# Queries, keys and latents of two attentions computed with tokens on the partitions, in a two-layer hybrid block

## The chip, the cores and the metric

The kernel runs on one core of a Trainium2 chip. The metric is device microseconds of one execution. A profiled execution gives busy times, waits and the granted TensorE clock. TensorE multiplies matrices; VectorE (DVE), ScalarE (ACT) and GpSimd (POOL) work elementwise; SyncE (SP) starts the weights' transfers and POOL's queue starts the others.

## The reference, cut to what matters

256 tokens, width 2048, float32. A first layer (forgetting attention and an RWKV scan) is followed by a second layer, the block that the change touches:

```python
h = rms_norm(x, norm_g)
proj = h @ w_in                     # split into c_q, c_kv, k_rope_raw, mem_q, conv parts, gates
q = (rms_norm(c_q, q_norm_g) @ w_uq).reshape(b, s, 16, 128 + 64)
q_nope = rms_norm(q[..., :128], qn_nope_g)
q_rope = apply_rope(rms_norm(q[..., 128:], qn_rope_g), cos, sin)
kv = (rms_norm(c_kv, kv_norm_g) @ w_ukv).reshape(b, s, 16, 128 + 128)
k_nope, v = rms_norm(kv[..., :128], kn_nope_g), kv[..., 128:]
k_rope = apply_rope(rms_norm(k_rope_raw, kn_rope_g), cos, sin)
p = softmax(where(allowed, (q_nope @ k_nope.T + q_rope @ k_rope.T) * scale, -inf))
# memory: 4 heads of 256
mq = rms_norm(mem_q.reshape(b, s, 4, 256), qn_g)
mk, mv = split(rms_norm(mem, mem_norm_g) @ w_mem_kv); mk = rms_norm(mk, kn_g)
x = x + merged @ w_o                # merged: the gated sum of convolution, MLA and memory
```

A norm here is over the 512 channels of a latent, the 128 or 64 of a head's part, or the 256 of a memory head.

## The kernel before

All weights stream from HBM in 658 blocks of 128x1024 in a fixed order (`weight_groups`, L27). For each block `conv_to` makes two copies, `whi` (ScalarE, L278) and `wlo = raw - whi` (VectorE, L241); activations are kept as such pairs too, and a product is three matmuls in fp32r: high by high, high by low, low by high. Four blocks of `whi`/`wlo` exist at a time, and they are made three blocks ahead of TensorE.

`gemm` (L478) runs one group, 512 output columns of a projection, over its k-tiles of 128. It has two forms. With `tm` set (tokens on the partitions) the activations of 128 tokens are the stationary operand and 512 weight columns stream: two accumulators, six matmuls of 128x512 per k-tile. Without it (channels on the partitions) 128 weight columns are stationary and 256 tokens stream: four accumulators, twelve matmuls of 128x256 per k-tile. All matmuls through the helper `mm` carry L286. Five banks of PSUM hold accumulators, three serve everything else (`bank`).

The small work is written as generators (`spawn`): `gemm` calls `pump` between its matmuls, which advances the jobs while a simple clock of the engines says that there is room; the compiler then orders each engine's queue. So norms and attention lie between the weight matmuls.

Before the change the groups `mk`, `cq`, `ckv`, `krope`, `mq`, `qr`, `qn` and `kn` have channels on the partitions. Their norms are then sums over partitions: `head_rs` (L603) splits the squares into a pair, sums with eight `hs` matmuls against selectors, takes the reciprocal root on 128x256 (`rsqrt`, eleven VectorE steps), and brings the factors to all partitions by a round trip through DRAM on POOL's queue (`hd`, then `hr`). `mem_norm` and `nope_norm` (L1563) multiply by it, `q_rope_all` (L1613) and `rope_job` also rotate: `rotate` copies half-rows across partitions by DMA (`rot`) and combines with tables `cos` and `sin`. `latent_job` (L1438) sums with `mm(ps, ones, r)` (`lss`). In the stretch after `mz` the memory attention (`ms`, softmax `mx` and `msm`, transposes `mpt`, `mpo`), the MLA heads (`ls`, `sm`, `lpt`, `lpo`) and the causal convolution (`cg`, its shifted copies `ul` by DMA, its weights `cw`) run as jobs between the groups.

Of the kernel before, what the change touches and what calls it, by code (L numbers as in the profile page):

```python
# [26 lines left out]
def weight_groups():  # L27
# [29 lines left out]
    for j in range(2):  # L57
        add(f"mk{j}", "w_mem_kv_2", 2048, _tiles(512 * j, 4))
# [22 lines left out]
    for b in range(2):  # L81
        add(f"mq{b}", w, 2048, _tiles(7232 + 512 * b, 4))
# [144 lines left out]
def hybrid_kernel(ctx: ExitStack, tc: tile.TileContext, io, out):  # L227
# [301 lines left out]
    def to_pair(x, pair, gain=None):  # L529

        for i in range(2):
# [14 lines left out]
            yield  # L546

# [55 lines left out]
    def head_rs(sq, which, scale, eps, op=ALU.add):  # L603
# [1214 lines left out]
```

## Time and profile before

| | us |
|---|---|
| median of 3 runs (range) | 2023.71 (2021.61 to 2027.49) |
| the profiled execution, its span | 2022.89, 2021.0 |
| the groups `mk` to `mq`, first matmul to last | 838.5 to 1031.5 |
| the heads' groups `qr`, `qn`, `kn` and their attention, first to last | 1077.9 to about 1660 |
| granted TensorE clock | 0.999 |

A page of the profile lists each engine's busy time, the chain of work that ended last, and groups of instructions. A row of a timeline has the start, the length, the engine, the line, the operation, out<-in, the shape and, in brackets, how long the engine had stood idle and for whom. Matmul lengths overlap; the step from start to start is what one costs.

### The profile page before, as it was taken

The page shows a single profiled execution, that of the slowest core. Times are in us where ns is not written, and L with a number is a line of the kernel's source. Part 1 is how long each engine was busy: PE and PEld are TensorE (multiplying, and loading weights), DVE is VectorE, ACT ScalarE, POOL GpSimd, SP SyncE. Part 2 cuts the span into 40 slices and gives each one's busy share as a digit, 9 for nine tenths or more (in the row PEclk, how much of TensorE's full clock was granted, in tenths as well). Part 3 has the DMA queues.
Part 4 walks back from the last instruction along what each step waited for, and adds up shares of the span by engine and source line. Part 5 has one row for each costly group of instructions (what it writes and reads, how often), then busy time and mean ns, then how long its engine had stood idle before and what let it go on. Part 6 is the DMA issues. An engine that isn't in the chain of part 4 may idle for free. (4 is left out here: it accounts for less than half of the span.)

```text
span 2021.0 us, 31907 instructions
## 1 busy us (share of the span) xinstructions
PE 2004.6 (99%) x12702; PEld 1778.0 (88%) x12702; DVE 1305.3 (65%) x2005; ACT 977.3 (48%) x1330; POOL 82.1 (4%) x149
## 2 busy tenths in 40 slices
PE   9999999999999999999999999999999999999999
PEld 9999999898778888899999888888888889988887
DVE  8776847878446568656856675575765755555554
ACT  6734445454444545555445445445545444444432
POOL 0002000020100000000000100100000000000000
PEclk9999999999999999999999999999999999999999
DMA  8454544536546666565555655565665555566564
GB/s 274 162 180 155 196 136 139 179 119 202 174 157 236 229 201 201 191 214 195 182 182 186 189 193 184 181 226 166 198 208 167 188 177 171 193 210 211 192 200 146
DMA packets 106820, 378.52 MB, mean 187 GB/s; under 512 B 13178, under 2 KB 14162, under 8 KB 106672
## 3 DMA queue, kind: packets, MB, share of 16 engines
q1 hardware_dynamic: 97136, 350.11, 52.5%
q0 software_dynamic: 9104, 25.78, 4.4%
q8 instruction: 99, 1.62, 0.3%
q10 hardware_dynamic: 432, 0.61, 0.1%
q14 instruction: 49, 0.40, 0.1%
HBM read 367.32 MB, written 5.86 MB: 185 GB/s over the span
## 5 line engine op out<-in xcount | busy, mean ns | idle before, releaser
L241 DVE TENSOR_TENSOR wlo<-raw,whi 128x1024 fp32r<-128x1024 f32 (+1 forms) x659 | 801.9, 1222 | 559.1 <-ACT whi L278 552.4
L278 ACT ACTIVATE whi<-raw 128x1024 fp32r<-128x1024 f32 (+1 forms) x659 | 695.3, 1058 | 828.7 <-PE acc.lo L286 51.1
L286 PE MATMUL acc.lz<-h2l,whi 128*128 128x256 f32 x256 | 72.5, 284 | 0.0
L286 PE MATMUL acc.lz<-h2h,whi 128*128 128x256 f32 x256 | 72.4, 283 | 0.0
L286 PE MATMUL acc.lz<-h2h,wlo 128*128 128x256 f32 x256 | 72.1, 284 | 0.0
L286 PE MATMUL acc.gm<-wlo,h2h 128*128 128x512 f32 x128 | 50.0, 391 | 1.1 <-DVE wlo L241 1.1
L286 PE MATMUL acc.gb<-wlo,hh 128*128 128x512 f32 x128 | 50.0, 390 | 0.6 <-DVE wlo L241 0.6
L286 PE MATMUL acc.ga<-whi,hl 128*128 128x512 f32 x128 | 50.5, 394 | 0.0
L286 PE MATMUL acc.ga<-wlo,hh 128*128 128x512 f32 x128 | 50.4, 394 | 0.0
L286 PE MATMUL acc.gc<-wlo,h2h 128*128 128x512 f32 x128 | 50.2, 392 | 0.0
L286 PE MATMUL acc.gm<-whi,h2l 128*128 128x512 f32 x128 | 50.2, 392 | 0.0
L286 PE MATMUL acc.gl<-wlo,h2h 128*128 128x512 f32 x128 | 50.1, 392 | 0.0
L286 PE MATMUL acc.gc<-whi,h2l 128*128 128x512 f32 x128 | 50.1, 391 | 0.0
L286 PE MATMUL acc.ga<-whi,hh 128*128 128x512 f32 x128 | 50.0, 392 | 0.0
L286 PE MATMUL acc.gl<-whi,h2h 128*128 128x512 f32 x128 | 50.0, 392 | 0.0
L286 PE MATMUL acc.wo<-wlo,mh 128*128 128x512 f32 x128 | 49.9, 390 | 0.0
L286 PE MATMUL acc.w<-wlo,mgh 128*128 128x512 f32 x128 | 49.9, 390 | 0.0
L286 PE MATMUL acc.w<-whi,mgh 128*128 128x512 f32 x128 | 49.9, 390 | 0.0
L286 PE MATMUL acc.gc<-whi,h2h 128*128 128x512 f32 x128 | 49.9, 390 | 0.0
L286 PE MATMUL acc.wo<-whi,ml 128*128 128x512 f32 x128 | 49.9, 390 | 0.0
L286 PE MATMUL acc.gl<-whi,h2l 128*128 128x512 f32 x128 | 49.8, 389 | 0.0
L286 PE MATMUL acc.w<-whi,mgl 128*128 128x512 f32 x128 | 49.8, 389 | 0.0
(658 smaller groups left out, 5894.5 us busy)
## 6 DMA issues: line engine op xcount, KB each, us to landing
raw<-in_W SPq DMA_DIRECT2D x657, 512.0 KB, 3.5
hr<-hd POOLq DMA_DIRECT2D x10, 512.0 KB, 5.4
hr<-hd POOLq DMA_DIRECT2D x12, 256.0 KB, 4.4
xr<-in_xtm POOLq DMA_DIRECT2D x4, 512.0 KB, 6.3
mt<-in_memT POOLq DMA_DIRECT2D x4, 512.0 KB, 7.0
xbd<-x1g POOLq DMA_DIRECT2D x4, 512.0 KB, 3.9
xo<-xbd POOLq DMA_DIRECT2D x4, 512.0 KB, 4.9
out_tm<-xo SPq DMA_DIRECT2D x8, 256.0 KB, 4.8
```

What stands on the lines that cost most here:

```text
L241: DVE.tensor_tensor(out=o, in0=a, in1=b, op=op)
L278: ACT.activation(out=o, in_=a, func=f, scale=scale, **kw)
L286: TE.matmul(o, lhsT=l, rhs=r, start=start, stop=stop)
```

## The change

The groups named above, but for `krope`, get the `tm` form. Their rows are evacuated by `evac_rows` as two 128x512 copies. A norm is `tm_norm`: squares on ScalarE, a VectorE reduction along the row, `rsqrt` on a few numbers per partition, a broadcast product. The result goes back to channels on the partitions by TensorE transposes (`to_channels`, for the latents the existing `to_pair`), which apply the gain while the bank is read. The rotation `turn` works along the row with tables `rope` that hold gain and scale. `krope` keeps its form, with 64 instead of 128 (doubled) weight columns, and `rope_job` transposes it to tokens and back.

```diff
-        add(f"mk{j}", "w_mem_kv_2", 2048, _tiles(512 * j, 4))
+        add(f"mk{j}", "w_mem_kv_2", 2048, _tiles(512 * j, 4), tm=True)
...
-    add("cq", w, 2048, _tiles(4096, 4))
-    add("ckv", w, 2048, _tiles(4608, 4))
-    add("krope", w, 2048, [[(5120, 64), (5120, 64)]])
+    add("cq", w, 2048, _tiles(4096, 4), tm=True)
+    add("ckv", w, 2048, _tiles(4608, 4), tm=True)
+    add("krope", w, 2048, [[(5120, 64)]])
...
-                [[(192 * (8 * (h // 2) + 2 * i + e) + 128, 64) for e in range(2)] for i in range(4)])
-        add(f"qn{h}", "w_uq_2", 512, [[(192 * (4 * h + i), 128)] for i in range(4)])
-        add(f"kn{h}", "w_ukv_2", 512, [[(256 * (4 * h + i), 128)] for i in range(4)])
+                [[(192 * (8 * (h // 2) + 2 * i + e) + 128, 64) for e in range(2)] for i in range(4)], tm=True)
+        add(f"qn{h}", "w_uq_2", 512, [[(192 * (4 * h + i), 128)] for i in range(4)], tm=True)
+        add(f"kn{h}", "w_ukv_2", 512, [[(256 * (4 * h + i), 128)] for i in range(4)], tm=True)
...
+        width = sum(n for t in e["tiles"] for _, n in t)
...
-                        wh = hi_t[b][:, i * cols:(i + 1) * cols]
-                        wl = lo_t[b][:, i * cols:(i + 1) * cols]
+                        wh = hi_t[b][:, i * cols:i * cols + width]
+                        wl = lo_t[b][:, i * cols:i * cols + width]
                         ah = pairs[k // 4][0][:, k % 4, 128 * t:128 * t + 128]
                         al = pairs[k // 4][1][:, k % 4, 128 * t:128 * t + 128]
-                        mm(acc[t], ah, wh, start=k == 0, stop=False)
-                        mm(acc[t], ah, wl, start=False, stop=False)
-                        mm(acc[t], al, wh, start=False, stop=k == kt - 1)
+                        o = acc[t][:, :width]
+                        mm(o, ah, wh, start=k == 0, stop=False)
+                        mm(o, ah, wl, start=False, stop=False)
+                        mm(o, al, wh, start=False, stop=k == kt - 1)
                         if i == per - 1:
                             pump()
                     if ks[-1][2] == kt - 1:
-                        evac(t, acc[t])
+                        evac(t, acc[t][:, :width])
...
+    def tm_norm(x, d, eps):
+        n = fsz(x) // d
+        v = x if len(x.shape) == 2 else x.rearrange("p t c -> p (t c)")
+        sq = a4("tsq").rearrange("p a b -> p (a b)")[:, :n * d]
+        act(sq, v, AF.Square)
+        r = b1("tn").rearrange("p (k n) -> p k n", k=4)[:, :, :n]
+        ms, y, t, g = (r[:, k, :] for k in range(4))
+        red(ms, sq.rearrange("p (n d) -> p n d", d=d), ALU.add)
+        yield
+        ts(ms, ms, 1.0 / d, ALU.mult, eps, ALU.add)
+        yield from rsqrt(ms, y, t, g)
+        yield SOFT
+        v = v.rearrange("p (n d) -> p n d", d=d)
+        mul(v, v, y.unsqueeze(2).to_broadcast([128, n, d]))
+        yield
+    def to_channels(x, dst, gain):
+        for i in range(2):
+            ps = bank("tc").rearrange("p (c t) -> p c t", c=2)
+            for c in range(2):
+                for t in range(2):
+                    o = 256 * i + 128 * c
+                    TE.transpose(ps[:, c, 128 * t:128 * t + 128], in_=x[:, t, o:o + 128], identity=cc("ident"))
+                    clock["pe"] += 0.11
+            yield
+            for c in range(2):
+                acopy(dst[:, 2 * i + c, :], ps[:, c, :], scale=gain(2 * i + c))
+            yield
+    def evac_rows(d, b, name):
+        t4 = tm4(out4(name))
+        d[b] = t4
+        return lambda t, ps: acopy(t4[:, t, :], ps)
...
-        gemm(f"mk{b}", memn, evac_copy(mk, b, "mk"))
+        gemm(f"mk{b}", memn, evac_rows(mk, b, "mk"))
     def mem_norm(d, gain):
-        sum4 = a4("mks")
         for b in range(2):
-            sq = a4("mksq")
-            act(sq, d[b], AF.Square)
-            yield
-            s4 = sq.rearrange("p (a c) b -> p a c b", c=2)
-            add(sum4[:, 2 * b:2 * b + 2, :], s4[:, :, 0, :], s4[:, :, 1, :])
-        yield from head_rs(sum4, 1, 1.0 / 256.0, 1e-6)
-        y = head_rs.out
-        for b in range(2):
-            t4 = d[b].rearrange("p (a c) b -> p a c b", c=2)
-            for c in range(2):
-                stt(t4[:, :, c, :], t4[:, :, c, :], gain(c), y[:, 2 * b:2 * b + 2, :], ALU.mult, ALU.mult)
-            yield
+            yield from tm_norm(d[b], 256, 1e-6)
+            t = a4("mc")
+            yield from to_channels(d[b], t, lambda c: gain(c % 2))
+            d[b] = t
...
+        gr = b1("gr").rearrange("p (k c) -> p k c", k=4)
         nc.gpsimd.dma_start(out=pos, in_=io["pos"])
-        yield from lag()
-        a, k, r = b1("ang"), b1("ak"), b1("ar")
-        vcopy(a, pos)
-        ts(a, a, cc("invf"), ALU.mult)
+        nc.gpsimd.dma_start(out=gr[:, 0:3, :], in_=io["ropeg"])
+        yield from lag(2 * LAG)
+        w = b1("ang").rearrange("p (k c) -> p k c", k=4)
+        a, k, r, pf = (w[:, i, :] for i in range(4))
...
+        act(r, r, AF.Sin)
+        act(k, k, AF.Sin)
+        ts(gr[:, 0, :], gr[:, 0, :], 192.0 ** -0.5, ALU.mult)
+        for i in range(2):
+            for j, tab in enumerate((k, r)):
+                for e in range(2):
+                    o = slice(32 * e, 32 * e + 32)
+                    mul(rope[:, i, j, :, o], tab.rearrange("p (t f) -> p t f", t=2),
+                        gr[:, i, o].unsqueeze(1).to_broadcast([128, 2, 32]))
+            yield
+    def turn(x, i, n):
+        v = x.rearrange("p t (n c) -> p t n c", c=64)
+        b = a4("turn").rearrange("p a b -> p (a b)")[:, :128 * n].rearrange("p (t n c) -> p t n c", t=2, c=64)
+        tab = lambda j: rope[:, i, j, :, :].unsqueeze(2).to_broadcast([128, 2, n, 64])
+        mul(b, v, tab(1))
+        mul(v, v, tab(0))
+        yield
+        sub(v[:, :, :, 0:32], v[:, :, :, 0:32], b[:, :, :, 32:64])
+        add(v[:, :, :, 32:64], v[:, :, :, 32:64], b[:, :, :, 0:32])
+        yield
...
     def latent_job(d, gain, name):
-        t = d[0]
-        ps = bank("lss")
-        sq = a4("lsq")
-        act(sq, t, AF.Square)
-        r = b1("lr")
-        fold(sq, r, 0)
-        yield
-        mm(ps[:, :256], ones, r)
-        yield
-        ms = b1("lms")
-        ts(ms, ps[:, :256], 1.0 / 512.0, ALU.mult, 1e-6, ALU.add)
-        y, tmp, g = b1("ly"), b1("lt"), b1("lg")
-        yield from rsqrt(ms, y, tmp, g)
-        for c in range(4):
-            stt(t[:, c, :], t[:, c, :], pc(gain, c), y, ALU.mult, ALU.mult)
-        yield
+        x = d[0]
+        yield from tm_norm(x, 512, 1e-6)
         p = new_pair(name)
-        split(t, p[0], p[1])
         lat[name] = [p]
+        yield from to_pair(x, p, lambda c: pc(gain, c))
...
-    def rope_job(x, n, gain, out):
...
+    def rope_job(x):
+        k = b1("kr").rearrange("p (t c) -> p t c", t=2)
+        ps = bank("kr")[:, 0:128]
+        for t in range(2):
+            TE.transpose(ps[:, 64 * t:64 * t + 64], in_=x[:, 128 * t:128 * t + 128], identity=cc("ident", 0, 64, 0, 64))
+            clock["pe"] += 0.11
+        yield
+        x = b1("krn")
+        acopy(x[:, 0:128], ps)
+        yield from tm_norm(x[:, 0:128], 64, 1e-6)
+        yield from turn(x[:, 0:128].rearrange("p (t c) -> p t c", t=2), 1, 1)
+        for e in range(2):
+            vcopy(k[:, :, 64 * e:64 * e + 64], x[:, 0:128].rearrange("p (t c) -> p t c", t=2))
...
-    def rotate(x, n, out):
-        s = a4("rot")[:, 0:n, :]
-        for e in range(4):
-            p = 32 * e
-            q = 32 * (e ^ 1)
-            POOL.dma_start(out=s[p:p + 32, :, :], in_=x[q:q + 32, :, :])
-        yield from lag()
-        cb = lambda a: a.unsqueeze(1).to_broadcast([128, n, 256])
-        mul(s, s, cb(sin))
-        yield
-        mul(x, x, cb(cos))
-        yield
-        add(out, x, s)
...
-    def nope_norm(t, gain):
-        sq = a4("nsq")
-        act(sq, t, AF.Square)
-        yield
-        yield from head_rs(sq, 1, 1.0 / 128.0, 1e-6)
-        stt(t, t, gain, head_rs.out, ALU.mult, ALU.mult)
-        yield
     def mla_job(g):
-        qt, kt_, o = qn[g], kn[g], a4("mo")
+        qt, kt_, o = a4("qc"), a4("kc"), a4("mo")
         lo[g] = o
-        yield from nope_norm(qt, qns[:, 0:1])
-        yield from nope_norm(kt_, pc("kn_g"))
+        for x, t, gain in ((qn[g], qt, qns[:, 0:1]), (kn[g], kt_, pc("kn_g"))):
+            yield from tm_norm(x, 128, 1e-6)
+            yield from to_channels(x, t, lambda c: gain)
...
-        t = qr.pop(g)
-        sq = a4("rsq")
-        act(sq, t, AF.Square)
-        yield
-        yield from head_rs(sq, 0, 1.0 / 64.0, 1e-6)
-        stt(t, t, qns[:, 1:2], head_rs.out, ALU.mult, ALU.mult)
-        yield
-        yield from rotate(t, 4, t)
-        yield
-        qr[g] = []
-        for e in range(2):
-            p, o = slice(64 * e, 64 * e + 64), slice(64 - 64 * e, 128 - 64 * e)
-            x = a4("qro", F32R)
-            acopy(x[p, :, :], t[p, :, :])
-            sub(x[o, :, :], t[p, :, :], x[p, :, :].bitcast(F32))
-            qr[g].append(x)
-            yield
+        x = qr.pop(g)
+        yield from tm_norm(x, 64, 1e-6)
+        yield from turn(x, 0, 8)
+        both = [a4("qro", F32R) for _ in range(2)]
+        for i in range(2):
+            ps = bank("tc").rearrange("p (c t) -> p c t", c=2)
+            for c in range(2):
+                for t in range(2):
+                    o = 256 * i + 128 * c
+                    TE.transpose(ps[:, c, 128 * t:128 * t + 128], in_=x[:, t, o:o + 128], identity=cc("ident"))
+                    clock["pe"] += 0.11
+            yield
+            cs = slice(2 * i, 2 * i + 2)
+            for e in range(2):
+                p, o = slice(64 * e, 64 * e + 64), slice(64 - 64 * e, 128 - 64 * e)
+                acopy(both[e][p, cs, :], ps[p, :, :])
+                sub(both[e][o, cs, :], ps[p, :, :], both[e][p, cs, :].bitcast(F32))
+            yield
+        qr[g] = both
...
-            gemm(f"qr{g // 2}", lat["cq"], evac_copy(qr, g // 2, "qr"))
+            gemm(f"qr{g // 2}", lat["cq"], evac_rows(qr, g // 2, "qr"))
             jq[g // 2] = spawn(q_rope_all(g // 2))
-        gemm(f"qn{g}", lat["cq"], evac_copy(qn, g, "qn"))
-        gemm(f"kn{g}", lat["ckv"], evac_copy(kn, g, "kn"))
+        gemm(f"qn{g}", lat["cq"], evac_rows(qn, g, "qn"))
+        gemm(f"kn{g}", lat["ckv"], evac_rows(kn, g, "kn"))
```

The order of the queues shows the move. On TensorE, at the latents: `lss` of the first latent stood among the 128x256 matmuls of `ckv` (`h2h`, `h2l`: the activations).

```order
L286 MATMUL acc.ckv_9870<-h2l_8847,whi_9863 128x256
L286 MATMUL acc.ckv_9870<-h2h_8846,wlo_9864 128x256
L286 MATMUL lss_9879<-lr_9882,one_84 128x256
L286 MATMUL acc.ckv_9871<-h2h_8846,whi_9863 128x256
L286 MATMUL acc.ckv_9871<-h2l_8847,whi_9863 128x256
```

The same place after the change (`con`: the identity):

```order
L286 MATMUL acc.ckv_9577<-whi_9637,h2l_8880 128x512
L286 MATMUL acc.ckv_9577<-whi_9637,h2h_8879 128x512
L538 MATMUL tr_9706<-con,cq_9351 128x128 x4
L286 MATMUL acc.ckv_9577<-wlo_9638,h2h_8879 128x512
L286 MATMUL acc.ckv_9577<-whi_9637,h2l_8880 128x512
```

The sum over partitions is gone, four transposes of the normed latent stand there, and the streams are twice as wide.

On VectorE, at the first memory head's softmax, before (`qr`: the rotated query part, `hr`: its factors from DRAM):

```order
L1153 TENSOR_REDUCE mx_11709<-ms_11685 128x1 x2
L261 SCALAR_TENSOR_TENSOR qr_11293<-qr_11293,qns,hr_11641 128x1024
L1158 RECIPROCAL mx_11709<-mx_11709 128x2
L255 TENSOR_SCALAR msm_11708<-msm_11708,mx_11709 128x256 x2
L241 TENSOR_TENSOR wlo_11715<-raw_11621,whi_11714 128x1024
```

And after (`tn`: the few numbers of a norm):

```order
L1191 TENSOR_REDUCE mx_11163<-ms_11121 128x1
L241 TENSOR_TENSOR tn_11129<-tn_11129 128x8
L257 TENSOR_SCALAR tn_11129<-tn_11129 128x8
L241 TENSOR_TENSOR tn_11129<-tn_11129 128x8
L241 TENSOR_TENSOR qn_10792<-qn_10792,tn_11129 128x1024
L241 TENSOR_TENSOR wlo_11171<-raw_11041,whi_11170 128x1024
L1196 RECIPROCAL mx_11163<-mx_11163 128x2
L255 TENSOR_SCALAR msm_11162<-msm_11162,mx_11163 128x256 x2
```

The product that needed `hr` no longer stands between `mx` and `msm`; the end of a norm's chain and one weight's `wlo` do.

On POOL's queue, up to the first convolution, before:

```order
L622 DMA hd_11501<-hy_11435 4x256
L623 DMA hr_11502<-hd_11501 128x1024
L625 DMA hd_11640<-hy_11575 8x256
L627 DMA hr_11641<-hd_11640 64x4x256 x2
L1495 DMA rot_11759<-qr_11293 32x1024 x4
L1522 MEMSET ul_12064 1x512
L1522 MEMSET ul_12065 2x512
L1525 DMA cw_12062<-in_cwt 128x1024
L1526 DMA cw_12063<-in_cwt 128x512
L1524 DMA ul_12064<-cg_11615 1x16x32
L1524 DMA ul_12065<-cg_11615 2x512
```

And after:

```order
L1441 DMA pos_9377<-in_pos 128x2
L1442 DMA gr_9378<-in_ropeg 128x192
L1546 MEMSET ul_11442 1x512
L1547 DMA ul_11442<-cg_10959 127x1024
L1548 DMA ul_11442<-cg_10959 1x16x32
L1546 MEMSET ul_11443 2x512
L1547 DMA ul_11443<-cg_10959 126x1024
L1548 DMA ul_11443<-cg_10959 2x512
L1549 DMA cw_11440<-in_cwt 128x1024
L1550 DMA cw_11441<-in_cwt 128x512
```

The round trips and the rotation's copies are gone, and `cw` now stands behind the four copies of `cg`.

More of the change, by code (lines that the diff above doesn't have):

```diff
@@ L505, in gemm @@
                     if ks[-1][2] == kt - 1:
-                        evac(t, acc[t])
+                        evac(t, acc[t][:, :width])
             else:
                 for c in range(nt):
-                    o = acc[c][:, :256]
+                    o = acc[c][0:min(128, width), :256]
                     for b, i, k in ks:
                         s = i * cols + 128 * c
-                        wh, wl = hi_t[b][:, s:s + 128], lo_t[b][:, s:s + 128]
+                        wh, wl = hi_t[b][:, s:s + o.shape[0]], lo_t[b][:, s:s + o.shape[0]]
                         ah, al = pairs[k // 4][0][:, k % 4, :], pairs[k // 4][1][:, k % 4, :]
@@ L1461, in hybrid_kernel @@
     KRl = [KRl2[:, e, :] for e in range(2)]
-    def rope_job(x, n, gain, out):
-        w = 256 * n
-        sq = b2("rsq")[:, :w]
-        act(sq, x, AF.Square)
-        yield
-        ps = bank("rss")[:, :w]
-        rr = a4("rss", F32R).rearrange("p a b -> p (a b)")
-        split(sq, rr[:, 0:w], rr[:, 512:512 + w])
+    def rope_job(x):
[4 more added lines that the diff above has]
+            clock["pe"] += 0.11
+        yield
+        x = b1("krn")
[4 more added lines that the diff above has]
+            vcopy(k[:, :, 64 * e:64 * e + 64], x[:, 0:128].rearrange("p (t c) -> p t c", t=2))
         yield
-        mm2(ps, sel("blk", 0, 128), rr[:, 0:w], rr[:, 512:512 + w])
+        ps = bank("kr")[:, 0:256]
+        for t in range(2):
+            TE.transpose(ps[:, 128 * t:128 * t + 128], in_=k[:, t, :], identity=cc("ident"))
+            clock["pe"] += 0.11
         yield
-        ms = b2("rms")[:, :w]
-        ts(ms, ps, 1.0 / 64.0, ALU.mult, 1e-6, ALU.add)
-        yield from rs512(ms, w)
-        stt(x, x, gain, rs512.out, ALU.mult, ALU.mult)
-        yield
-        r3 = lambda t: t.rearrange("p (a b) -> p a b", a=n)
-        yield from rotate(r3(x), n, r3(out))
-        yield
-        acopy(KRh, out)
+        acopy(KRh, ps)
         DVE.memset(KRl2.bitcast(F32), 0.0)
@@ L1486, in rope_job @@
             p = slice(64 * e, 64 * e + 64)
[L1487 to L1502 removed]
+            sub(KRl[e][p, :], ps[p, :], KRh[p, :].bitcast(F32))
     jl2 = []
[L1505 removed]
+    gemm("cq", h2, evac_rows(cq, 0, "cq"))
     jl2.append(spawn(latent_job(cq, "qg", "cq")))
[L1507 removed]
+    gemm("ckv", h2, evac_rows(ckv, 0, "ckv"))
     jl2.append(spawn(latent_job(ckv, "kvg", "ckv")))
[L1509 removed]
+    krt = b1("krt")[0:64, 0:256]
     gemm("krope", h2, lambda c, ps: acopy(krt, ps))
[L1511 removed]
+    jl2.append(spawn(rope_job(krt)))
     oc = []
@@ L1710, in hybrid_kernel @@
     for b in range(2):
[L1711 removed]
+        gemm(f"mq{b}", h2, evac_rows(mq, b, "mq"))
     for b in range(2):
@@ L1801 @@
         "memT": channel_major(a["mem_2"]),
-        "pos": np.ascontiguousarray(np.broadcast_to(a["positions_2"].reshape(1, 256), (128, 256))),
+        "pos": np.ascontiguousarray(a["positions_2"].reshape(2, 128).T),
+        "ropeg": np.ascontiguousarray(np.broadcast_to(np.stack(
+            [a["mla_qn_rope_g_2"].reshape(64), a["mla_kn_rope_g_2"].reshape(64),
+             np.tile(np.power(10000.0, -np.arange(32) / 32).astype(np.float32), 2)])[None], (128, 3, 64))),
         "params": pack_params(a),
```

22 lines of the change are left out of this document (8 added, 14 removed).

## The prediction

> **What bounds the kernel now.** I read the page's busy times first, then the chain that ended last, then what TensorE waited for in the stretch that the change touches (830 to 1660 us).
>
> ```profile
> span 2021.0 us, 31907 instructions
> PE 2004.6 (99%) x12702; PEld 1778.0 (88%) x12702; DVE 1305.3 (65%) x2005; ACT 977.3 (48%) x1330; POOL 82.1 (4%) x149
> PE 44%; DMA 1%; DVE 0%; ACT 0%; issue 0%; DVEq 0%; ACTq 0%
> ```
>
> The second row gives each engine's busy time; the third is the head of the chain, which holds almost nothing but TensorE. So the time is a sum over TensorE's queue: what is taken from it or put into it counts in full, and what VectorE, ScalarE and the DMAs do counts only where TensorE waits for them. These are all its waits between 830 and 1660 us:
>
> ```profile
> PE mpt L1674 <- DVE msm L255: 1.6, 1, 1.6
> PE acc.gm L286 <- DVE wlo L241: 1.1, 1, 1.1
> PE acc.kn L286 <- ACT qn L278: 0.3, 1, 0.3
> ```
>
> Three waits, 3.0 us in all. The reason for the first two is in VectorE's timeline:
>
> ```profile
> 1113.82 0.76 DVE L1153 TENSOR_REDUCE mx<-ms 128x1 f32<-128x256 f32 x2 [0.80 <-PE ms L286]
> 1120.84 1.28 DVE L261 SCALAR_TENSOR_TENSOR qr<-qr,qns,hr 128x1024 f32<-128x1024 f32 x1 [6.27 <-DMA hr<-hd]
> 1122.23 0.61 DVE L255 TENSOR_SCALAR msm<-msm,mx 128x256 f32<-128x256 f32 x2
> 1425.86 1.28 DVE L261 SCALAR_TENSOR_TENSOR qr<-qr,qns,hr 128x1024 f32<-128x1024 f32 x1 [3.49 <-DMA hr<-hd]
> ```
>
> VectorE stood 6.27 us (then 3.49 us) at a product that needs `hr`, the head norms' factors coming back from DRAM. Behind it in its queue stood `msm` in the one place and a weight's `wlo` in the other, and TensorE ran dry. Note the cover: of 6.27 us held, 1.6 reached TensorE.
>
> **The main term: 512 columns in one stream.** Two stretches do the same work in the two forms: `mv` (two groups of 16 k-tiles by 512 columns, tokens on the partitions) and `mz` (the same size, channels on the partitions). The start times of one matmul after the other, first and last of ten us:
>
> ```profile
> 899.79 0.39 PE L286 MATMUL acc.mv<-whi,memnh 128*128 128x512 f32 x1
> ...
> 909.99 0.39 PE L286 MATMUL acc.mv<-whi,memnh 128*128 128x512 f32 x1
> 1039.79 0.28 PE L286 MATMUL acc.mz<-h2h,wlo 128*128 128x256 f32 x1
> ...
> 1049.99 0.28 PE L286 MATMUL acc.mz<-h2h,whi 128*128 128x256 f32 x1
> ```
>
> 45 steps of `mv` take 10.20 us, 226.7 ns each; 85 steps of `mz` take 10.20 us, 120.0 ns each. (The durations 0.39 and 0.28 overlap; only starts can be added.) One 512-wide matmul replaces two 256-wide ones and saves 240.0 - 226.7 = 13.3 ns. How many: `mk` and `mq` are two groups of 16 k-tiles each, `cq` and `ckv` one each, 96 k-tiles; `qr` (2 groups), `qn` and `kn` (4 each) have 4 k-tiles, 40 together. 136 k-tiles x 4 column tiles x 3 = 1632 matmuls become 816. **816 x 13.3 ns = -10.9 us.**
>
> `krope` keeps its 48 matmuls, with 64 instead of 128 columns as the stationary operand. No row shows that form. If a step follows the columns loaded it is 60 ns, -2.9 us; if the load, 192 ns long in every 256-wide row, were no longer hidden, +3.5 us. The array streams the same 256 columns, so I take 0, the row it is nearest to.
>
> The Trainium skill's page "TensorE: Matmul & The Clock Gate" (section "Wait — 56ns, not 53.3ns?") gives a back-to-back step of N / 2.4 GHz plus about 2.5 ns. By it a pair would save 2.5 ns and the whole 816 only some 2 us, an estimate from that page; the two rows above show 13.3 ns, and the measurement decides.
>
> **Norms and transposes on TensorE.** The head norms summed squares over the partitions with matmuls; now a reduction along the row does it, and the normed rows are transposed back.
>
> ```profile
> 1154.15 0.95 PE hs L286 x8
> 1132.93 0.86 PE ms L286 x4
> 1144.48 0.44 PE mpt L1674 x4
> L286 PE MATMUL lss<-lr,one x4: 377/377/378, 965.8 to 986.1; 128*128 128x256 f32 x4
> L286 PE MATMUL rss<-rss,conr x2: 281/282/282, 1003.6 to 1005.1; 128*128 128x256 f32 x2
> ```
>
> The first three rows are pieces of the chain, start and length. Gone: 12 calls of `head_rs` with 8 `hs` each, 12 x 0.95 = 11.4; the latents' `lss`, 4 records of the same plain-fp32 256-wide kind as `ms` (0.86 for four), 0.9; two `rss` at 0.12, 0.2. Together **-12.5 us**. Added: 96 transposes in `to_channels` (12 tiles of 8), 16 in `q_rope_all`, 16 in the two latents' `to_pair`, 4 in `rope_job`: 132. Four take 0.44 us as `mpt`, so **+14.5 us**. The nearest other row, `tr`, runs closer:
>
> ```profile
> 852.73 0.38 PE L536 MATMUL tr<-con,hx 128*128 128x128 f32 x2
> 852.87 0.37 PE L286 MATMUL acc.mk<-memnh,whi 128*128 128x256 f32 x1
> 853.08 0.82 PE L536 MATMUL tr<-con,hx 128*128 128x128 f32 x6
> 853.65 0.36 PE L286 MATMUL acc.mk<-memnl,whi 128*128 128x256 f32 x1
> ```
>
> Eight transposes and one 0.12 us matmul fill 852.73 to 853.65: 0.10 each, 13.2 us for 132. I take 14.5, since most new groups are fours like `mpt`.
>
> **VectorE and ScalarE lie beside this.** These rows give the price per norm of 128x1024:
>
> ```profile
> L241 DVE TENSOR_TENSOR sql<-nsq,sqh 128x1024 fp32r<-128x1024 f32 x8 | 9.8, 1222 | 0.7 <-ACT sqh L278 0.3 <-PE acc.mo L286 0.2 <-PE acc.kv L286 0.2
> L261 DVE SCALAR_TENSOR_TENSOR qn<-qn,qns,hr 128x1024 f32<-128x1024 f32 x4 | 5.1, 1284 | 10.6 <-DMA hr<-hd 10.6
> L257 DVE TENSOR_SCALAR hms<-hs 128x256 f32<-128x256 f32 x12 | 5.1, 421 | 3.9 <-PE hs L286 3.9
> L1153 DVE TENSOR_REDUCE mx<-ls 128x1 f32<-128x256 f32 x15 | 6.2, 415 | 0.0
> L1158 DVE RECIPROCAL mx<-mx 128x2 f32<-128x2 f32 x19 | 3.1, 162 | 5.6 <-ACT sm L278 5.6
> L278 ACT ACTIVATE sqh<-nsq 128x1024 fp32r<-128x1024 f32 x8 | 8.4, 1054 | 9.0 <-DVE qn L261 4.7 <-DVE mg L261 4.2
> L278 ACT ACTIVATE h2h<-tr,par 128x256 fp32r<-128x256 f32 x16 | 7.0, 470 | 5.0 <-PE tr L536 2.8 <-DVE h2l L261 2.1
> ```
>
> Removed: the split's 1.22, the product's 1.28, and twelve 256-wide steps of the reciprocal root at up to 0.42, some 4.5: 7.0 us. Added: a product of 1.22; a reduction over 1024, which no row shows (between one and four times the 0.42 over 256, so 1.7 at most); and the same twelve steps on 2 to 16 numbers, between nothing and 0.42 each, by the nearest row, the reciprocal on 2 numbers, 0.16: 1.9. That is 4.8, so VectorE gets about 2 us lighter per norm. ScalarE loses a split of 1.05 and gains four scaled reads of a bank at 0.47, +0.8 per norm, and is busy 48%. The rotation trades three 1024-wide products and sums for two and two halves. All of this costs nothing as long as the weights' `whi` and `wlo` are built ahead of TensorE (three blocks of 12 steps, 3 x 2.7 us); beyond that lead each us late would be a us of the kernel.
>
> **Waits that go and waits that may come.** POOL's queue loses the 10 + 2 round trips `hd`/`hr` and the 12 `rot` copies and gains one load, `ropeg`; SP's order is the same row for row. So two of the three waits above lose their cause, `hr`; the third, `kn` on the evacuation of `qn`, goes because a group now holds two of the five accumulator banks instead of four: **-3.0 us**. What is late next? The transposes stand in TensorE's queue behind a VectorE chain (reduction, twelve steps, product), but that chain holds no DMA, and like the old chain it is built some three weight blocks ahead. The one DMA left in VectorE's way is the convolution's: in the first convolution `cw` now stands behind the four `ul` copies on POOL, which wait for `cg`, where it used to be loaded ahead. The second convolution had this order already:
>
> ```profile
> 1304.53 0.55 POOL L1523 DMA_DIRECT2D ul<-cg  x1
> 1307.05 0.58 POOL L1525 DMA_DIRECT2D cw<-in_cwt  x1
> 1316.93 2.50 DVE L241 TENSOR_TENSOR ul<-ul,cw 128x512 f32<-128x512 f32 x4 [2.45 <-DMA cw<-in_cwt]
> DMA to landing us min/median/max: 4.1/7.4/11.7
> ```
>
> `cw` followed 2.5 us behind the first copy, VectorE was held 2.45 us, and no wait of TensorE stands there. By these rows `cw` lands 2.5 + 7.4 = 9.9 us after `cg` (6.6 to 14.2). Behind the held product stand, in the first convolution, the third memory head's `mx` and `msm` and two weights' `wlo`; `mpt` and `cb` wait for those. A hold of 2.45 us cost nothing, one of 6.27 cost 1.6: nothing to 1.6 at each convolution and at a few norms with a short lead; I take **+1.0** for all, with 0 and 6 (four waits like the longest) as ends.
>
> **Sum.** -10.9 - 12.5 + 14.5 - 3.0 + 1.0 = -10.9. The profiled execution took 2022.9 us around its span of 2021.0, and the median shown is 2023.7, 0.8 higher: 2022.9 - 10.9 = **2012.0 us**.
>
> **Rivals.**
> *New waits eat it.* The normed rows come late for their transposes or `mpt`. Without any new wait the sum gives 2011; five waits of the 1.6 us seen once make it 2019, no difference that can be told. For it: 33 new groups of transposes each depend on another engine. Against it: in 730 us the old order, with as many such places, shows one wait (0.3 us) that no DMA caused. Chance 0.12.
> *The wide stream saves nothing here*, because what the 256-wide form loses is a wait for weight loads that the changed groups keep. PEld is busy through all of `mz` (46.40 of 46.40 us) and not of `mv`:
>
> ```profile
> 888.10:931.50 43.40, 43.40 (x194) 35.98 (x193) 21.92 (x20) 21.66 (x23) 0.00 (x0) 1.00 0.59 194
> 1031.50:1077.90 46.40, 46.40 (x389) 46.40 (x388) 23.11 (x25) 22.14 (x26) 0.00 (x0) 1.00 0.55 181
> ```
>
> (PE busy, PEld busy, DVE, ACT, POOL, clock.) With 0 to 2 us in place of 10.9 it ends at 2021 to 2023. Against it: `mv` has just the form that the groups get. Chance 0.04. The 2.5 ns of the skill's page above would give this result too; the trace does not agree.
> *Transposes at their full length: slower.* If each of the 132 held the array for its recorded length instead of its 0.11 us step,
>
> ```profile
> L536 PE MATMUL tr<-con,hx x32: 270/272/273, 852.7 to 871.5; 128*128 128x128 f32 x32
> ```
>
> they would cost 132 x 0.272 = 35.9 instead of 14.5, and the kernel would take 2012.0 + 21.4 = 2033 us. It loses from 0.11 + 10.9/132 = 0.19 us per transpose, and measurably from 0.24. Against it: the four of `mpt` in 0.44 us. Chance 0.05. The Trainium skill's same page (Part 4, "PE-mode transpose") gives about 275 ns for one in a kernel; the trace agrees on the length (272 ns) and not on the step (0.10 to 0.11 us).
>
> **How the numbers follow.** Forecast 0.79, the waits 0.12, the stream 0.04, slower 0.05. A measurement of this kernel can tell about 0.3%, 6 us, from no change; the forecast is faster by more, the first two rivals lie within it: faster 0.79, same 0.16, slower 0.05. Low end: transposes at 0.10 (-1.3), no new wait (-1.0), `krope` at half (-2.9): 2006.8. High end: waits of 6 (+5.0) and `krope` with open loads (+3.5): 2020.5, which takes in most of the first rival.
>
> **What would show it.** In the changed profile, steps of 227 ns in `mk`, `cq`, `ckv`, `mq`, `qr`, `qn` and `kn`; groups of four `tc` in 0.44 us; 11916 matmul records; no `hr` behind the head norms; TensorE's waits from 830 to 1660 us near 1 us. A wait of `tc` or `mpt` on `tn`, `msm` or a weight's `wlo`, or a `tc` step of 0.2 us, would prove me wrong.

## The result and the profile after

| | us |
|---|---|
| before, median (range) | 2024.51 (2021.61 to 2027.49, 4 runs) |
| after, median (range) | 2012.11 (2010.67 to 2012.98, 4 runs) |
| after, the profiled execution, its span | 2012.98, 2011.2 |

The ratio after to before is 0.9938, with a 95% interval of 0.9926 to 0.995: the medians lie 12.4 us (0.6%) apart. The forecast was 2012.0.

The page of the changed kernel: span, busy times, head of the chain.

```profile
span 2011.2 us, 30300 instructions
PE 1996.2 (99%) x11916; PEld 1736.4 (86%) x11916; DVE 1276.6 (63%) x2039; ACT 985.3 (49%) x1344; POOL 61.5 (3%) x112
PE 96%; DVE 2%; DMA 1%; issue 1%; ACT 0%; POOL 0%; SPq 0%; DVEq 0%; POOLq 0%
```

TensorE still sets the end. It has 11916 records, as many as forecast; VectorE is 28.7 us lighter, ScalarE 8.0 heavier. The longest waits of TensorE in the changed kernel, over the whole run (what waits, for what, us in total, times, the longest):

```profile
PE acc.vr L286 <- DVE wlo L241: 2.6, 1, 2.6
PE lora L286 <- ACT xgh L278: 1.7, 1, 1.7
PE acc.gb L286 <- DVE wlo L241: 1.7, 1, 1.7
```

All lie outside the stretch from 820 to 1650 us, and in that stretch the view is empty: the three waits of before are gone and nothing has come in their place.

To compare runs I use windows that begin at the first matmul of `mk`, where the changed work begins, since the unchanged 839 us ahead of it differ by some 3 us from run to run. Each window is that of the one profiled execution of its run. Before, the stretch from `mk` to the first matmul of `lz`, from there to the end, and both together (window, length, then busy us of PE, PEld, DVE, ACT, POOL with their records, granted clock, DMA share, GB/s):

```profile
838.70:1656.80 818.10, 815.16 (x4753) 722.83 (x4752) 536.22 (x826) 405.60 (x561) 31.59 (x58) 1.00 0.58 190
1656.80:2021.00 364.20, 359.89 (x1976) 314.16 (x1974) 192.13 (x227) 153.14 (x180) 2.15 (x4) 1.00 0.58 188
838.70:2021.00 1182.30, 1175.05 (x6727) 1036.99 (x6725) 728.35 (x1052) 558.75 (x741) 33.74 (x62) 1.00 0.58 190
```

And after:

```profile
840.60:1649.80 809.20, 809.20 (x3990) 682.87 (x3989) 509.56 (x875) 415.22 (x582) 11.57 (x22) 1.00 0.56 183
1649.80:2011.20 361.40, 357.15 (x1953) 311.40 (x1951) 190.73 (x216) 151.19 (x173) 2.16 (x4) 1.00 0.58 189
840.60:2011.20 1170.60, 1166.35 (x5941) 994.27 (x5939) 700.29 (x1090) 566.41 (x755) 13.73 (x26) 1.00 0.57 185
```

From `mk` to the end the change saves 1182.3 - 1170.6 = **11.7 us**: 8.9 ahead of `lz`, and 2.8 behind it, where before the last MLA head's attention (23 matmul records) still ran beside `lz`. The spans differ by 9.8 only because `mk` began 1.9 us later in this profiled execution.

### The profile page after: what moved, and what is told of

Read it like the earlier page. It is cut to its first block, busy times and chain, and to the rows that moved or that the text cites. A ratio compares the mean times of both kernels' runs of the same rounds, so it can differ in the third digit from the quotient of the medians.

```text
span 2011.2 us, 30300 instructions
## 1 busy us (share of the span) xinstructions
PE 1996.2 (99%) x11916; PEld 1736.4 (86%) x11916; DVE 1276.6 (63%) x2039; ACT 985.3 (49%) x1344; POOL 61.5 (3%) x112
## 4 chain that ended last, share of the span: by engine, by line
PE 96%; DVE 2%; DMA 1%; issue 1%; ACT 0%; POOL 0%; SPq 0%; DVEq 0%; POOLq 0%
PE acc.lz L286 5%; PE acc.ga L286 4%; PE acc.gc L286 4%; PE acc.gm L286 4%; PE acc.gl L286 4%; PE acc.wo L286 4%; PE acc.w L286 4%; PE acc.lo L286 4%; PE acc.gb L286 4%; PE acc.fq L286 2%; PE acc.r L286 2%; PE acc.mz L286 2%; PE acc.fk L286 2%; PE acc.zb L286 2%; PE acc.pf L286 2%; PE acc.vr L286 2%
## 5 line engine op out<-in xcount | busy, mean ns | idle before, releaser
L286 PE MATMUL acc.gm<-whi,h2h 128*128 128x512 f32 x128 | 50.1, 392 | 0.0
```

What stands on the lines that cost most here:

```text
L286: TE.matmul(o, lhsT=l, rhs=r, start=start, stop=stop)
```

## The experiments

Below, "from `mk` to the end" is always that window; before has 1182.3 and after 1170.6.

### The changed kernel once more

> The changed kernel itself, beside the three others on the same chip: 2010.7 to 2013.0 us, ratio 0.994.

Measured: 2013.41 us (2011.21 to 2014.42), 0.4 above the range expected, ratio 0.9945 (0.9931 to 0.996), and the window has 1170.6 us again, to the tenth. Here the window repeats better than the whole time, so I use it for terms of 1 to 3 us. (Where TensorE waits it repeats less well: a kernel below that was profiled twice differs by 1.0 us. The kernel before was profiled once.)

### The wide stream undone

```diff
-        add(f"mk{j}", "w_mem_kv_2", 2048, _tiles(512 * j, 4), tm=True)
+        add(f"mk{j}", "w_mem_kv_2", 2048, _tiles(512 * j, 4))
...
-        return lambda t, ps: acopy(t4[:, t, :], ps)
+        return lambda c, ps: acopy(x[:, c, :], ps)
```

The same for `cq`, `ckv`, `mq`, `qr`, `qn` and `kn`; norms, rotation and transposes stay as changed.

> The changed kernel with only the wide streams undone: mk, cq, ckv, mq, qr, qn and kn run with channels on the partitions again (1632 matmuls of 128x256 for 816 of 128x512), while evacuation, row norms, rotation and transposes stay as changed. The rows then hold channels where tokens are meant, so the norms run over the wrong axis and the output is not the reference's. My theory (each pair of narrow matmuls costs 13.3 ns more than one wide one): 10.9 us more than the changed kernel, 2012.1 + 10.9 = 2023.0 us, steps of 120 ns in these groups. Rival (the gain came from the norms, the round trips and the waits that went, the stream saves nothing or 2.5 ns a pair): 2012 to 2014 us.

Measured: 2021.93 us (2020.67 to 2023.64), ratio to before 0.9987 (0.9978 to 0.9996). The window:

```profile
839.90:2020.50 1180.60, 1176.35 (x6757) 1037.73 (x6755) 699.64 (x1090) 568.60 (x787) 13.70 (x26) 1.00 0.56 184
```

It has 816 matmul records more than after and takes 10.0 us more: the wide stream is worth 10.0 us here, and nearly the whole gain. (The whole times, beside the repeat on the same chip, differ by 8.5 us; they carry the differences ahead of `mk` too.) What is left of the change, norms, transposes and `krope` with the three waits gone, is worth 1182.3 - 1180.6 = 1.7 us. The 0.9 missing from 10.9 may lie in the transposes. The stretch of `mk` holds only matmuls and 32 of the old transposes `tr`; first with narrow streams (this run), then with wide ones (after):

```profile
839.90:889.40 49.50, 49.50 (x417) 49.47 (x416) 36.57 (x68) 28.16 (x47) 3.23 (x6) 1.00 0.65 215
```

```profile
840.60:887.90 47.30, 47.30 (x226) 39.21 (x225) 36.79 (x68) 27.58 (x43) 3.23 (x6) 1.00 0.66 225
```

Taking 384 matmuls of 0.120 from 49.5 us leaves 0.107 for each of 32 transposes, taking 192 of 0.2267 from 47.3 us leaves 0.119. Over 132 transposes the difference is 1.6 us; that it is the cause was not shown by itself.

### The wide stream alone

```diff
-        add(f"mk{j}", "w_mem_kv_2", 2048, _tiles(512 * j, 4))
+        add(f"mk{j}", "w_mem_kv_2", 2048, _tiles(512 * j, 4), tm=True)
...
-        gemm(f"mk{b}", memn, evac_copy(mk, b, "mk"))
+        gemm(f"mk{b}", memn, evac_rows(mk, b, "mk"))
```

This is the kernel before with 512 columns streamed in the seven kinds of group. Its norms still go over the partitions, which now hold tokens, so its sums are not those of the reference.

> The kernel before with only the wide streams: the same seven kinds of groups in the token form, 816 matmuls of 128x512; norms by selectors, round trips through DRAM and rotation by DMA stay, and run over the wrong axis, so the output is not the reference's. My theory: 10.9 us less than before, 2024.5 - 10.9 = 2013.6 us, with VectorE still held by hr and one to three us of waits of TensorE. Rival (the norms made the gain): 2022 to 2025 us.

Measured: 2018.24 us (2014.59 to 2020.68), ratio 0.9964 (0.995 to 0.9978); window 1177.5, so 4.8 us gained where 10.9 were taken off TensorE: between the theory (2013.6) and the rival (2022 to 2025), a miss for both. Its waits of TensorE between 820 and 1650 us:

```profile
PE mpt L1680 <- DVE msm L255: 3.1, 1, 3.1
PE acc.cb L286 <- DVE wlo L241: 2.2, 1, 2.2
```

5.3 us instead of 3.0. TensorE gets to these places sooner than what they wait for does: counted from `mk`'s first matmul, TensorE ran dry ahead of `mpt` 5.2 us earlier than before, and the product that needs `hr` began 3.6 us earlier. VectorE's timeline shows it standing longer than before at the same two kinds of product (6.27 and 2.45 before).

```profile
1119.85 1.28 DVE L261 SCALAR_TENSOR_TENSOR qr<-qr,qns,hr 128x1024 f32<-128x1024 f32 x1 [7.18 <-DMA hr<-hd]
...
1309.37 2.50 DVE L241 TENSOR_TENSOR ul<-ul,cw 128x512 f32<-128x512 f32 x4 [4.36 <-DMA cw<-in_cwt]
```

And there is a second loss, behind the wait, in TensorE's timeline:

```profile
1118.13 0.39 PE L286 MATMUL acc.cg<-wlo,h2h 128*128 128x512 f32 x1
1121.66 1.17 PE L1680 MATMUL mpt<-con,msm 128*128 128x128 f32 x4 [3.14 <-DVE msm L255]
...
1123.05 0.63 PE L286 MATMUL acc.cg<-whi,h2h 128*128 128x512 f32 x1
...
1124.76 0.56 PE L286 MATMUL acc.cg<-wlo,h2h 128*128 128x512 f32 x1
```

Four steps from 1123.05 to 1124.76 take 0.43 us each, where the same matmul took 0.23 ahead of the wait. The granted clock says why, in the windows around the two waits:

```profile
1115.00:1130.00 15.00, 11.86 (x48) 9.48 (x47) 6.75 (x9) 5.83 (x7) 2.16 (x5) 0.89 0.63 190
1312.00:1330.00 18.00, 16.95 (x71) 14.04 (x72) 17.83 (x29) 5.71 (x6) 0.00 (x0) 0.91 0.61 196
```

If the slow steps count as half speed, 0.89 over 15 us is 3.3 us of it, 0.91 over 18 us is 3.2 us; each costs half of that, 3.3 us together. The sum: -10.9 + 2.3 + 3.3 = -5.3, against -4.8 measured; with the 10.0 of the run before this one it is -4.4. So the parts of the change do not add up from each side: alone, the stream brings 4.8; on top of the norms it brings 10.0, where VectorE has no `hr` to stand at and no wait of TensorE is left.

The Trainium skill, page "TensorE: Matmul & The Clock Gate" (Part 1, "The HAM clock gate"), states that the clock halves after an idle window of about 3.4 us and is whole again after a busy one of that length. The length of the slow stretch agrees (3.2 to 3.3 us); the waits right ahead of it, 3.1 and 2.2 us, were shorter than the page's window, and there the measurement decides.

### The stream alone again, and with the convolution's weights early

The chain of waits led `cb`'s wait to `cw`, the convolution's weights, and not to `hr`. Two runs side by side test that: the same kernel once more, and with the loads moved from behind the `ul` copies to the place ahead of `cg`'s matmuls:

```diff
     def conv_groups(b):
+        w = [tm4(a4("cw")) for _ in range(2)]
+        POOL.dma_start(out=w[0], in_=io["cwt"][:, b, 0:2, :])
+        POOL.dma_start(out=w[1][:, 0, :], in_=io["cwt"][:, b, 2, :])
         g = tm4(out4("cg"))
...
-        jc = spawn(conv_job(b, g), True)
+        jc = spawn(conv_job(b, g, w), True)
```

> The wide stream alone once more, as the neighbour of the run above and to see how steady its two waits are. If they are set by the order of the program: mpt 3.1 and cb 2.2 within 0.5 us, and 1177.5 within 1 us from the first mk matmul to the end. If they hang on how the DMAs fall: either may be missing, and the time from mk's start then is down to 1171.

> The wide stream alone on the kernel before (norms still over partitions, so they take their sums over the wrong axis), and the convolution's weights cw loaded before cg's matmuls instead of behind the ul copies. Theory (of the two TensorE waits of the stream alone, cb's 2.2 us came from cw landing 13.5 us after its issue, mpt's 3.1 us from hr): cb's wait goes and with it the slow matmuls behind it; from the first mk matmul to the end 1177.5 becomes about 1174; mpt's wait stays at 2 to 3.5 us. Rival (cb's wait also comes from an hr product ahead of it): cb's wait stays at 1 us or more, 1176 to 1178.

TensorE's waits of the repeat:

```profile
PE mpt L1680 <- DVE msm L255: 2.5, 1, 2.5
PE ls L286 <- DVE kn L261: 1.6, 1, 1.6
PE acc.cb L286 <- DVE wlo L241: 1.2, 1, 1.2
PE acc.gm L286 <- DVE wlo L241: 0.2, 1, 0.2
```

and with the weights early:

```profile
PE mpt L1680 <- DVE msm L255: 2.7, 1, 2.7
PE ls L286 <- DVE kn L261: 1.4, 1, 1.4
```

The repeat has 5.5 us of waits and a window of 1176.5 (span 2015.8, `mk` at 839.3): in these two profiles the sum of the waits is nearly the same, its places are not, which neither expectation said. With `cw` early `cb`'s wait is gone and the window is 1174.8 (2013.4 - 838.6), as expected; what is left stands behind products that VectorE held for `hr` (6.9 and 5.5 us). The clock fell around `mpt` alone in both runs, to 0.91 over 18 us, another 1.6 us each. With 10.0 for the stream the sums are -10.0 + 2.5 + 1.6 = -5.9 for the repeat and -10.0 + 1.1 + 1.6 = -7.3 with the weights early; the windows give -5.8 and -7.5. So alone, too, the stream takes about 10 us off TensorE's queue, and waits and slow matmuls give a part back. The whole times, 2016.76 (ratio 0.9958, 0.9942 to 0.9974) and 2015.46 (0.996, 0.9944 to 0.9975), do not tell the two apart. The stream alone with the `hr` holds taken away as well was not tried.

### Every new transpose twice

```diff
-                    TE.transpose(ps[:, c, 128 * t:128 * t + 128], in_=x[:, t, o:o + 128], identity=cc("ident"))
-                    clock["pe"] += 0.11
+                    for _ in range(2):
+                        TE.transpose(ps[:, c, 128 * t:128 * t + 128], in_=x[:, t, o:o + 128], identity=cc("ident"))
+                        clock["pe"] += 0.11
```

In `to_channels` and `q_rope_all`, 112 of the 132.

> The changed kernel with each of the 112 tc transposes issued twice into the same place; the result is the same. My theory (a transpose costs its step, 0.11 us): +12.3 us, 2012.1 + 12.3 = 2024.4 us. Rival (it holds the array for its recorded 0.272 us): +30.5 us, 2042.6 us. If transposes were hidden somewhere: 2012 us.

Measured: 2024.35 us (2022.69 to 2025.9), ratio to before 0.9998 (0.9989 to 1.0007). The window:

```profile
838.20:2020.80 1182.60, 1178.40 (x6053) 1006.68 (x6052) 698.86 (x1090) 567.20 (x755) 13.76 (x26) 1.00 0.56 183
```

112 records more and 12.0 us more than after: 0.107 us per transpose. (Each extra one stands right behind its twin, so what a step into or out of a group costs is not in it.) The slower rival, 0.272 each or 30.5 us, falls, and so does the one that they are hidden. Transposes alone would give the gain back if there were twice as many.

### A DRAM round trip in the row norms

```diff
-        yield SOFT
+        s = dpool.tile([128, 16], F32, name=nm("nd"), tag="nd", bufs=4)
+        z = tiny("nr", 16)[:, :n]
+        POOL.dma_start(out=s[:, :n], in_=y)
+        POOL.dma_start(out=z, in_=s[:, :n])
+        yield from lag(2 * LAG)
+        y = z
```

The factors of every row norm go to DRAM (`nd`) and back (`nr`), as the old head norms' did, but 2 to 16 numbers per partition, where `hr` filled 128x1024.

> The changed kernel with a round trip through DRAM put back into each row norm: the factors (2 to 16 numbers per partition) go out and come back on POOL's queue, with the same lag as before, ahead of the broadcast product. Nothing else differs. My theory (TensorE's waits came from VectorE standing at a product whose factors are in flight): VectorE waits of 2 to 6 us for nr at most of the norms, and TensorE waits of 1 to 5 us in all between 820 and 1650 us, 2013 to 2017 us. Rival (the waits came from VectorE's load, which is lighter now): TensorE waits stay at 0.0 in that stretch, 2012 us.

Measured: 2013.23 us (2011.92 to 2015.24), ratio 0.9943 (0.9924 to 0.9962). VectorE's waits for it, two of the seven groups:

```profile
DVE mq L241 <- DMA nr<-nd: 8.9, 2, 4.8
...
DVE mk L241 <- DMA nr<-nd: 6.2, 2, 5.4
```

The only wait of TensorE in the stretch:

```profile
PE mpt L1698 <- DVE msm L255: 0.3, 1, 0.3
```

VectorE is held fourteen times, for up to 5.4 us, and TensorE waits 0.3 us; the window is 1171.7, 1.1 more than after, of which 0.7 lie behind `lz`, where no wait stands. The expectation was a miss: a hold as such reaches TensorE hardly at all. The longer holds in this study, and what of them reached TensorE: at `ls` 5.5 us 1.4 and 6.1 us 1.6; at `mpt` 5.3 us 0.3, 6.27 us 1.6, 6.9 us 2.7, 7.2 us 2.5 and 3.1; at `cb` 2.45 us nothing, 3.9 us 1.2, 4.4 us 2.2; at `gm` 3.49 us 1.1 before, and 6.3 us 0.2 in the repeat of the stream alone. So a hold has a cover, and only what goes beyond it counts; the cover was 4 to 5 us at `mpt` and `ls`, 2 to 3 us at `cb`, and anything from 2.4 to 6.1 us at `gm`.

### What keeps `cw` late: three loads ahead of it

All three on the changed kernel, in `conv_job` ahead of the `ul` copies, into a buffer nobody reads: a load that waits for nothing; a copy of `cg`; the old `hd`/`hr` pair, fed from `cg`.

```diff
+        POOL.dma_start(out=tm4(a4("hx")), in_=io["cwt"][:, b, 0:2, :])
...
+        POOL.dma_start(out=tm4(a4("hx")), in_=u)
...
+        d = dpool.tile([8, 256], F32, name=nm("hd"), tag="hd", bufs=4)
+        POOL.dma_start(out=d[0:4, :], in_=u[0:128:32, 0, 0:256])
+        POOL.dma_start(out=a4("hr"), in_=d[0:4, :].unsqueeze(0).to_broadcast([128, 4, 256]))
```

> The changed kernel with one more load of 512 KB on POOL in each convolution, ahead of the four ul copies, into a buffer that nobody reads; nothing else. It stands where the head norms' hr load stood in the kernel before. Theory (the hr loads also held back the convolution's weights, by sharing the DMA engines, and that is why the changed kernel's cw lands early): in the second convolution cw lands 13 us after its issue, not 9.0, the held product ul waits 3 to 5 us, not 0.3, and TensorE gets a wait of 0 to 2.2 us between 820 and 1660 us; from the first mk matmul to the end 1170.6 becomes 1170.6 to 1174. Rival (cw is as late as its place behind the ul copies makes it, and hr's transfer has no part): cw at 9 to 10 us, ul held under 1 us, no TensorE wait, 1170.6.

> As the run with the idle load, but the extra 512 KB is a copy of cg, which has to wait for cg and so is issued right ahead of the ul copies, where the idle load went out some 35 us earlier. Nobody reads it. Theory (the transfer that the head norms put there delays the convolution's weights): in the second convolution cw lands 11 to 14 us after its issue, not 9.0; ul is held 2 to 5 us, not 0.3; TensorE waits 0 to 2.2 us there; 1170.6 to 1174 from the first mk matmul to the end. Rival (hr's transfer has no part in it): cw lands after 9 to 10 us, ul held under 1 us, no wait, 1170.6.

> As the run with the copy ahead, but in its place stands the very pair that a head norm of the kernel before put there: 4 KB written to DRAM (hd) and read back to 128 partitions, 512 KB (hr), both behind cg and ahead of the ul copies on POOL; nobody reads it. The plain copy of 512 KB landed after 3.0 us, hr in the kernel before after 6 to 7. Theory (hr is a slow transfer and what stands behind it in POOL's queue lands late): cw lands 12 to 14 us after its issue, the copies ul after 9 to 12, the product ul is held 3 to 6 us (with the 2.5 us by which the pair puts off the copies), TensorE waits 0 to 2.2 us; 1170.6 to 1174 from the first mk matmul to the end. Rival (hr has no part in how late cw lands; the stream alone met a busier time of the weights' loads): cw at 9 to 10.5 us, the product held 0 to 3 us by the later issue alone, no TensorE wait.

The load that waits for nothing was issued 15 us before the copies in the first convolution and 50 us before them in the second, landed after 3.7 and 4.5 us, and so tests nothing (2012.81 us, window 1170.7, `cw` after 9.2 us). The other two were timed once each (2010.47 and 2012.67 us). The DMA issues of the second convolution, KB each and us to landing, after:

```profile
cw<-in_cwt POOLq DMA_DIRECT2D x1, 512.0 KB, 9.0
```

the changed kernel once more:

```profile
cw<-in_cwt POOLq DMA_DIRECT2D x1, 512.0 KB, 10.0
```

with the copy ahead:

```profile
hx<-cg POOLq DMA_DIRECT2D x1, 512.0 KB, 3.0
cw<-in_cwt POOLq DMA_DIRECT2D x1, 512.0 KB, 9.6
```

with the pair ahead:

```profile
hr<-hd POOLq DMA_DIRECT2D x1, 512.0 KB, 6.6
cw<-in_cwt POOLq DMA_DIRECT2D x1, 512.0 KB, 10.8
```

and the stream alone:

```profile
hr<-hd POOLq DMA_DIRECT2D x1, 512.0 KB, 7.1
cw<-in_cwt POOLq DMA_DIRECT2D x1, 512.0 KB, 13.5
```

The changed kernel by itself spreads from 9.0 to 10.0, and the kernel before, with `hr` ahead of the copies, has 9.8. So the copy's 9.6 says nothing, and the pair's 10.8 lies 0.8 above that spread; in the first convolution `cw` landed sooner with the pair (6.5 us) than without it (8.1). That `hr` makes `cw` late is not shown. With the pair the product `ul` is held 2.5 and 2.3 us in the two convolutions, no wait of TensorE follows, and the window stays at 1170.7 (with the copy 1170.6): the rival's side, but for `cw`'s 10.8. What makes `cw` as late as 13.5 us in the stream alone (12.4 in its repeat) stays open.

### The stationary columns of `krope`

`krope`'s 16 k-tiles with 128, 96, 64 and 32 weight columns loaded, four k-tiles each; each narrower quarter leaves rows out of the sum.

```diff
+                        if name == "krope":
+                            o = acc[c][0:(128, 96, 64, 32)[k // 4], :256]
...
```

> The changed kernel with krope's stationary operand 128, 96, 64 and 32 columns wide for four k-tiles (12 matmuls) each, 256 columns streamed in all; the other rows of these k-tiles are left out of the sum, so krope's output is not the reference's. If the 13.3 ns above 256 / 2.4 GHz that a step shows are a fixed cost per matmul, all four quarters step at 120 ns; if they follow the columns loaded, 120, about 116, about 113 and about 110 ns. The whole kernel: 2012 us either way.

First and last of the twelve matmuls of three of the widths, in TensorE's timeline (one execution, 2011.82 us):

```profile
976.56 0.28 PE L286 MATMUL acc.krope<-h2h,whi 128*128 128x256 f32 x1
977.87 0.28 PE L286 MATMUL acc.krope<-h2h,wlo 128*128 128x256 f32 x1
...
979.38 0.28 PE L286 MATMUL acc.krope<-h2h,whi 128*64 128x256 f32 x1
980.64 0.28 PE L286 MATMUL acc.krope<-h2h,wlo 128*64 128x256 f32 x1
980.75 0.28 PE L286 MATMUL acc.krope<-h2h,whi 128*32 128x256 f32 x1
982.00 0.28 PE L286 MATMUL acc.krope<-h2h,wlo 128*32 128x256 f32 x1
```

One step, as the mean of eleven: 119.1 ns with 128 columns, 116.4 with 96, 114.5 with 64, 113.6 with 32; the starts are read to 0.01 us, so each may be off by about 1 ns. Four times fewer columns save 5.5 ns of a step. Neither theory as written: the step is nearly fixed, a small part follows the columns loaded.

## Why the prediction was right, and where it was not

**The bound.** Right: time is TensorE's queue, and the window of after has no wait of TensorE ahead of `lz`.

**The stream, -10.9.** Right: 10.0 on top of the other parts. The chain of the changed kernel shows the step at work, 36 matmuls of 512 columns in 8.16 us, 0.227 each, and the fours of `tc` in 0.44:

```profile
931.55 8.16 PE acc.cq L286 x36
939.72 0.44 PE tc L574 x4
```

Starts instead of durations, and a pair of like stretches, made it so. That the kernel would gain it in full only with the norms changed too was not in the prediction; alone the stream brought 4.8.

**Norms gone -12.5, transposes +14.5.** Right: 132 x 0.107 = 14.1 for the transposes, or 14.5 by the chain's 0.44 for four. From start to start in the trace of before, the 96 `hs` took 12.0, the four `lss` 0.5 and the two `rss` 0.2: 12.7. The prediction had 11.4 for `hs` and 0.9 for `lss`, the latter from the row of `ms`, a kind that steps more slowly (0.17 us against 0.12); the two errors nearly cancel. The run with the stream undone agrees: 1.7 + 14.1 - 3.0 - 0.3 (`krope`) = 12.5.

**Three waits gone, -3.0.** Right, the view is empty. The reason given for the third, `kn`'s 0.3 (two accumulator banks instead of four), is not what it took: with the stream undone a group holds four banks again, and the wait is gone there too. What ended it is not shown.

**New waits, +1.0.** The term that was mis-sized: 0. The 7.4 us to landing was the median over two unlike cases, 4.1 and 5.0 for the loads issued ahead of the copies and 9.8 and 11.7 for those behind them; only the latter are like the new order, in which the four loads took 8.1 to 9.9. `cw` landed 11.6 us behind the first copy in the second convolution, where 9.9 was taken, and still the product was held for 0.3 us (1.3 in the repeat), not 2.45; in the first convolution VectorE stood 0.4 ahead of it:

```profile
1288.14 1.22 DVE L241 TENSOR_TENSOR wlo<-raw,whi 128x1024 fp32r<-128x1024 f32 x1 [1.50 <-ACT whi L278]
1289.66 2.50 DVE L241 TENSOR_TENSOR ul<-ul,cw 128x512 f32<-128x512 f32 x4 [0.30 <-DMA cw<-in_cwt]
```

VectorE came to it later, with a weight's `wlo` done first. And a hold of that size would have cost nothing either: with the pair ahead it was 2.5 and 2.3 us, and no wait followed. The error made the forecast of the saving 1.0 too small.

**`krope`, 0.** Right within 0.3: from its first matmul to its last 5.33 us, against 5.64 before (979.17 to 984.81). The widths' 119.1 and 114.5 ns give 0.2 for 48 steps.

```profile
977.81 0.28 PE L286 MATMUL acc.krope<-h2h,whi 128*64 128x256 f32 x1
983.14 0.28 PE L286 MATMUL acc.krope<-h2h,wlo 128*64 128x256 f32 x1
```

**VectorE and ScalarE beside this.** Right: VectorE became 28.7 us lighter and ScalarE 8.0 heavier, and in the changed stretch no wait of TensorE tells of either.

**The sum.** The terms as the runs show them are -10.0 - 12.7 + 14.1 - 3.0 - 0.3 = -11.9, and the window has -11.7; the forecast was -10.9. That the median of 2012.11 lies 0.1 from the 2012.0 forecast is luck: the 2022.9 it was taken from is 1.6 below the 2024.51 measured beside it, and the saving of 12.4 is 1.5 above the forecast.

**Rivals.** New waits eating the gain: refuted by the empty view. The stream saving nothing: refuted by undoing it. Transposes at full length: refuted by doubling them.

## What to carry to other kernels

Where one engine sets the end, price a change by steps from start to start of like rows in the trace, and measure it from the first changed instruction on. Price a stall by what exceeds the cover behind it: here fourteen holds of up to 5.4 us cost 0.3 and one of 7.2 cost 3.1, and 1.6 more because the clock dropped behind the wait. The cover differs from place to place, so read it where the hold is. A faster bound engine runs into the late work of the others, so a saving on it and the removal of a hold belong together: here 4.8 us and 1.7 us from each side alone, and 11.7 us together.

## What the runs showed of the hardware

The steps of 120.0 ns (256 columns streamed) and 226.7 ns (512) lie 106.7 apart, so 13.3 ns of each do not grow with the columns. The Trainium skill, page "TensorE: Matmul & The Clock Gate" (section "Wait — 56ns, not 53.3ns?"), has about 2.5 ns beyond the columns; the runs here speak against it for this kernel's matmuls, each of which loads its stationary operand anew. With 32 stationary columns 113.6 ns are left of 119.1, so 5.5 of the 13.3 follow the columns loaded from 128 down to 32.

Some waits of TensorE cost another 1.6 us at a lower clock, and their length alone does not decide it. The same wait at `acc.vr`, ahead of the changed part, was 2.5 us in the kernel before and 2.6 us after. The granted clock over the ten microseconds around it, before and then after:

```profile
145.00:155.00 10.00, 7.51 (x51) 7.30 (x50) 9.88 (x19) 1.06 (x1) 0.00 (x0) 0.83 0.35 113
```

```profile
145.00:155.00 10.00, 7.45 (x63) 7.23 (x62) 9.88 (x18) 2.12 (x4) 0.00 (x0) 1.00 0.44 151
```

Before, the 256-wide steps went from 0.12 to 0.21 us some 1.1 us after the wait had ended, and stayed there for 3.4 us; after, they stayed at 0.12. Around `mpt`'s 2.5 us in the repeat of the stream alone the clock was 0.91 over 18 us. The waits of 1.6 us (`mpt` before) and 1.7 us (`acc.gb` after) left it at 1.00.

Reading 4 KB from DRAM into 128 partitions (`hr`, 512 KB in all) took 5.0 to 6.3 us in the kernel before, 5.1 and 6.6 with the pair ahead and up to 7.1 in the stream alone; a plain copy of the same size, from `cg`, took 3.0 and 3.7.
